# A gated two-mixer decoder layer on one core: which units of a gate block are seven-product units, how far ahead units are split, in how many steps a unit is rounded, and where token sums stand in the queues

## The chip, the cores and the metric

The kernel runs on one core of one Trainium2 chip. The metric is the device time of one execution in microseconds (us); lower is better. The kernel before takes 1052.6 us, the median of 3 runs (1051.69 to 1054.95).

## The reference

One decoder layer on 256 tokens of width 2048, all in float32. With `h` the normalised input, `proj = h @ w_in` is cut into the parts of two token mixers and two sets of merge gates:

```python
attn = attention(q, k, v) * silu(z_mla);          y_mla  = attn @ w_o_mla
conv = causal_conv(c_gate * c_in)                 # three taps
y_conv = (b_gate * conv * silu(z_conv)) @ w_o_conv
merged = sigmoid(g_mla) * y_mla + sigmoid(g_conv) * y_conv
out = x + rmsnorm(merged @ w_out) * g
```

`g_mla` and `g_conv` are each a product of the 256 x 2048 input with a 2048 x 2048 matrix of weights. The change is about these two products, the *gate stage*, and about the work shortly ahead of it.

## The kernel before, in words

**Numbers as pairs.** Every float32 operand is held as a rounded part and a remainder. ScalarE (ACT in the profile) makes the rounded copy, and VectorE (DVE) subtracts it from the source to get the remainder (`split_act`: lines 268 and 269). A product is three matmuls: high by high, high by low, low by high (`product`).

**Units.** The weights come as a list of units of 128 x 2048 numbers, one MB each, numbered in the order of use. SyncE (SP) loads them into three buffers `raw`. ACT writes `whi`, DVE writes `wlo`, each with three buffers; TensorE (PE) reads those. So `whi` of unit j goes where that of unit j - 3 was, and can be written when PE has finished unit j - 3. `raw` of unit j is loaded when DVE has done the remainder of unit j - 3. `take(i)`, called where PE's work on unit i is written, first calls `ahead`: it writes down loads and splits of the units that follow. In the gate stage and up to the last column block of the output it goes two units ahead with splits, elsewhere one.

**Order.** Matmuls, and those instructions that are wrapped in `keep_in_program_order`, keep the order in which the code is written, each on its engine. Everything else is placed by a scheduler of the framework, which may move an instruction forward in its engine's queue where another is expected to be ready later. Each engine then works its queue strictly in that order.

**Heads.** For each of 16 heads `h` (0 to 15) PE runs the scores of the head (`sc`), four units of convolution channels (`channels(h, 0..3)`, tile `cv`), the attention values of the head before (`o`), and every other head the queries and keys of the next pair of heads (`qn`, `kn`). At the end of `channels(h, 3)` the PSUM banks `cv` are read by ACT and DVE (`cv_w` or `cv_f`, lines 731 to 736).

**Token sums.** `token_sums` (lines 782 to 798), called in head 13 behind the keys of heads 14 and 15, adds and subtracts slices of the input (`xf`, six DVE instructions) and splits the four results (`xs`). The gate stage reads `xs`.

**Gate stage.** It has four blocks: `n` is the gate, `b` the half of its columns. A block has eight units, and a unit is of one of two kinds. A *whole* unit needs 24 matmuls (eight products). A *pair* unit needs seven products, 21 matmuls, by a scheme of the Strassen-Winograd kind: for it `split_pair` makes three sums of weight blocks on DVE: `tf` (1024 wide), `raw` (512 wide, it overwrites the first quarter of the raw unit), `tf` again (512 wide), at line 212. Then come the rounded copy and the remainder of the unit itself (`whi`, `wlo`) and of the three sums (`thi`, `tlo`, one buffer each). PE's products on a pair unit go in the order 7, 5, 1, 6, 4, 2, 3: the first two read `thi` and `tlo`, and product 4, the fifth in order, is the last that reads them. `gate_kinds` says which of the eight places is which: blocks 1 to 3 have pairs at places 0, 2, 4; block 0 has them at places 2, 4, 6.

After the last pair of a block ACT copies two product banks (`p1`, `p5`) and DVE forms the sums `u`. At the end of the block DVE adds and ACT applies the sigmoid (`sg`, lines 980 and 981).

Of the kernel before, what the change touches and what calls it, by code (L numbers as in the profile page):

```python
# [11 lines left out]
F32 = mybir.dt.float32  # L12
F32R = mybir.dt.float32r
I32 = mybir.dt.int32
AF = mybir.ActivationFunctionType
# [8 lines left out]
H = 16  # L24
# [60 lines left out]
def tile_layer(ctx: ExitStack, tc: tile.TileContext, xw, x, pos, pvec, post_g, wc, wz, wcv, wkr, wqk, wqr, wv, cwr, wsq, wg, out):  # L85
# [118 lines left out]
    def split_pair(i, t, hi, lo):  # L204

        raw = t[:, :].rearrange("p (b c) -> p b c", b=4)
        tf = d0.tile([P, 2, 3, S], F32, name=f"tf{i}", tag="tf", bufs=1)[:, :, :, :].rearrange("p a b c -> p (a b c)")
        tf = tf.rearrange("p (b c) -> p b c", b=3)
        thi, tlo = (d1.tile([P, 3, 512], F32R, name=f"t{o}{i}", tag=f"t{o}", bufs=1) for o in ("hi", "lo"))

        def tt(*a, op):
            tc.keep_in_program_order(nc.vector.tensor_tensor(*a, op=op))
# [54 lines left out]
    def split_act(hi, lo, src, keep=False):  # L267
        a = nc.scalar.activation(hi, src, AF.Copy)  # L268
        b = nc.vector.tensor_tensor(lo, src, hi.bitcast(F32), op=ALU.subtract)  # L269
        if keep:  # L270

            tc.keep_in_program_order(a)
            tc.keep_in_program_order(b)
# [508 lines left out]
    def token_sums(pool):  # L782


        both = x_both[:, :, :].bitcast(F32).rearrange("p (g k) c -> p g k c", k=STEP)[:, :2, :PAIRS]
        xs = pool.tile([P, 4, PAIRS, 2, P], F32R, name="xs")
        xf = pool.tile([P, 2, PAIRS, S], F32, name="xf", tag="tf", bufs=1)
        tt = nc.vector.tensor_tensor
        for g in range(2):
            tt(xf[:, g], both[:, g, :, :S], both[:, g, :, S:], op=ALU.add)  # L790
        (a11, a21), (a12, a22) = [[xf[:, g, :, t * P : (t + 1) * P] for t in range(NT)] for g in range(2)]
        tt(a22, a21, a22, op=ALU.add)
        tt(a21, a11, a21, op=ALU.subtract)
        tt(a11, a22, a11, op=ALU.subtract)
        tt(a12, a12, a11, op=ALU.subtract)
        for i, f in enumerate((a22, a11, a21, a12)):
# [12 lines left out]

    dstack = main.enter_context(ExitStack())  # L810

    for h in range(H):
        v, at = divmod(h, HV)

# [50 lines left out]
        if at and h < H - 1:  # L865
            arrive()
        channels(h, 2)
        if at == 0:
            arrive()
            if v:  # L870
                coming.append(channels_join(v - 1, 0))
# [6 lines left out]
        if h == H - 3:  # L878
            lstack.close()
            d0 = dstack.enter_context(tc.tile_pool(name="d0", bufs=1))  # L880
            xs = token_sums(d0)
        channels(h, 3)
        if at == 0:
            while coming:
                arrive()
# [50 lines left out]
    def gate_block(n, b, last):  # L936
# [17 lines left out]
        for i, (kind, ks) in enumerate(kinds):  # L954
            if last:
                for v in {6: (0, 1), 7: (2,)}.get(i, ()):
                    split_branch(v)
            w = take(units[i])
            if kind == "pair":
                for m in TAGS:  # L960
                    if m:
                        add_to(m, side(m, ks[0]), w[m], i, True)
            else:
                for m, t, half in ((2, 0, 0), (3, 0, 1), (4, 1, 0), (0, 1, 1)):
                    for j, k in enumerate(ks):
                        a = [x_both[:, k, o + t * P : o + (t + 1) * P] for o in (0, S)]
                        add_to(m, a, w(2 * j + half, 512), i, j == len(ks) - 1)
            if i == last_pair:
                p1, p5 = wide("p1"), wide("p5")
# [134 lines left out]

def gate_kinds():

    pairs = [("pair", (k, k + STEP)) for k in range(PAIRS)]
    paired = {k for _, ks in pairs for k in ks}
    rest = [k for k in range(KD) if k not in paired]
    plain = [("whole", ks) for ks in zip(rest[::2], rest[1::2])]  # L1110
    alternate = []
    for i, pair in enumerate(pairs):
        alternate += [pair, plain[i]]
    alternate += plain[PAIRS:]
    late = plain[-2:] + [u for u in alternate if u not in plain[-2:]]
    return {(n, b): late if n == b == 0 else alternate for n in range(2) for b in range(2)}


def _cols(w):
# [99 lines left out]
```

## Time and profile before

| | |
|---|---|
| median of 3 runs | 1052.6 us |
| the profiled execution | 1052.53 us |
| its span, first to last instruction | 1050.7 us |
| DVE busy | 743.0 us, 71% |
| ACT busy | 532.5 us, 51% |
| matmuls recorded | 4658 |
| granted PE clock, mean | 0.991 |
| gate stage on PE | 606.65 to 781.69 us of the span |

A row of a timeline has the start in us, the duration in us, the engine, the line, the operation, what is written and read, the shapes, and how many such instructions follow one another; in brackets stands how long the engine was idle and what ended that. Matmuls are pipelined: one of 128 x 512 has a duration of 0.39 us, and the next can start 0.23 us after it, so delays are read from the distance between starts. A row of grouped instructions has the count, the busy time, the mean duration in ns, and the idle time ahead of them with what ended it. A row of waits has total us, times, longest.

### The profile page before, as it was taken

The page shows a single profiled execution, that of the slowest core. Times are in us where ns is not written, and L with a number is a line of the kernel's source. Part 1 is how long each engine was busy: PE and PEld are TensorE (multiplying, and loading weights), DVE is VectorE, ACT ScalarE, POOL GpSimd, SP SyncE. Part 2 cuts the span into 40 slices and gives each one's busy share as a digit, 9 for nine tenths or more (in the row PEclk, how much of TensorE's full clock was granted, in tenths as well). Part 3 has the DMA queues.
Part 4 walks back from the last instruction along what each step waited for, and adds up shares of the span by engine and source line. Part 5 has one row for each costly group of instructions (what it writes and reads, how often), then busy time and mean ns, then how long its engine had stood idle before and what let it go on. Part 6 is the DMA issues. An engine that isn't in the chain of part 4 may idle for free.

```text
span 1050.7 us, 12467 instructions
## 1 busy us (share of the span) xinstructions
PE 1026.5 (98%) x4658; PEld 852.6 (81%) x4658; DVE 743.0 (71%) x960; ACT 532.5 (51%) x675; POOL 180.7 (17%) x345
## 2 busy tenths in 40 slices
PE   9999999999999999999998999899999999999997
PEld 7887888888888888888886878688888888888885
DVE  7578759677687767777776799788885545666562
ACT  7766546455555455564553545555564433333451
POOL 7621220204212142112312220000000000232000
PEclk9999999999999999999998999899999999999998
DMA  8754765668666685765765765455555555677842
GB/s 337 295 199 177 257 212 212 226 214 275 197 243 195 226 284 199 244 216 203 264 231 196 248 216 186 165 194 202 200 206 195 199 200 192 220 252 247 330 160 80
DMA packets 41948, 231.00 MB, mean 220 GB/s; under 512 B 7520, under 2 KB 8224, under 8 KB 18976
## 3 DMA queue, kind: packets, MB, share of 16 engines
q1 hardware_dynamic: 29808, 197.54, 52.8%
q0 software_dynamic: 11648, 29.38, 9.1%
q10 hardware_dynamic: 432, 3.29, 0.8%
q8 instruction: 36, 0.59, 0.2%
q14 instruction: 24, 0.20, 0.0%
HBM read 214.48 MB, written 11.53 MB: 215 GB/s over the span
## 4 chain that ended last, share of the span: by engine, by line
PE 83%; DVE 9%; issue 4%; ACT 2%; DMA 1%; SPq 0%; DVEq 0%; ACTq 0%
PE cv L90 28%; PE sq L90 17%; PE g L90 10%; PE z L90 8%; PE out L90 8%; DVE wlo L269 4%; PE qn L90 2%; PE ckv L90 2%; ACT whi L268 2%; PE kn L90 2%; PE qa L90 2%; PE vv L90 2%; PE sc L90 1%; PE o L90 1%; DVE tlo L269 1%
## 5 line engine op out<-in xcount | busy, mean ns | idle before, releaser
L269 DVE TENSOR_TENSOR wlo<-raw,whi 128x1024 fp32r<-128x1024 f32 (+2 forms) x290 | 423.5, 1485 | 229.0 <-ACT whi L268 228.4
L268 ACT ACTIVATE whi<-raw 128x1024 fp32r<-128x1024 f32 (+2 forms) x292 | 357.3, 1259 | 373.8 <-PE sq L90 96.9
L90 PE MATMUL cv<-whi,x_both 128*128 128x512 f32 x1024 | 324.1, 391 | 2.7 <-DVE cv_w L736 2.7
L90 PEld LDWEIGHTS cv<-whi,x_both 128*128 128x128 f32 x1024 | 192.9, 188 | 43.1 <-DVE cv_w L736 3.7
L90 PE MATMUL cv<-wlo,x_both 128*128 128x512 f32 x512 | 200.2, 391 | 0.0
L90 PE MATMUL g<-whi,x_both 128*128 128x512 f32 x368 | 119.8, 390 | 0.0
L90 PEld LDWEIGHTS cv<-wlo,x_both 128*128 128x128 f32 x512 | 96.4, 188 | 18.8
L90 PEld LDWEIGHTS g<-whi,x_both 128*128 128x128 f32 x368 | 69.5, 189 | 14.6
L90 PE MATMUL z<-whi,x_both 128*128 128x512 f32 x256 | 80.6, 390 | 0.0
L90 PE MATMUL sq<-whi,x_both 128*128 128x512 f32 x256 | 79.0, 389 | 0.0
L90 PE MATMUL sq<-whi,cv_both 128*128 128x512 f32 x256 | 79.0, 389 | 0.0
L90 PE MATMUL out<-whi,x_both 128*128 128x512 f32 x256 | 79.0, 389 | 0.0
L355 POOL DMA_DIRECT2D far<-via x64 | 35.3, 559 | 225.8 <-DVE via L348 224.8
L90 PE MATMUL g<-wlo,x_both 128*128 128x512 f32 x184 | 71.8, 390 | 0.0
L355 POOL DMA_DIRECT2D far<-sg x32 | 17.5, 552 | 311.5 <-DVE sg L1025 270.2
L90 PEld LDWEIGHTS sq<-whi,x_both 128*128 128x128 f32 x256 | 48.0, 188 | 10.0
L90 PEld LDWEIGHTS sq<-whi,cv_both 128*128 128x128 f32 x256 | 48.0, 188 | 9.9
L90 PEld LDWEIGHTS out<-whi,x_both 128*128 128x128 f32 x256 | 48.0, 188 | 9.9
L90 PEld LDWEIGHTS z<-whi,x_both 128*128 128x128 f32 x256 | 48.1, 188 | 9.9
L90 PE MATMUL z<-wlo,x_both 128*128 128x512 f32 x128 | 49.8, 389 | 0.0
L90 PE MATMUL sq<-wlo,x_both 128*128 128x512 f32 x128 | 49.8, 389 | 0.0
L90 PE MATMUL sq<-wlo,cv_both 128*128 128x512 f32 x128 | 49.8, 389 | 0.0
(242 smaller groups left out, 1327.6 us busy)
## 6 DMA issues: line engine op xcount, KB each, us to landing
raw<-wcv_dram SPq DMA_DIRECT2D x64, 1024.0 KB, 5.4
raw<-wsq_dram SPq DMA_DIRECT2D x48, 1024.0 KB, 4.8
raw<-wg_dram SPq DMA_DIRECT2D x32, 1024.0 KB, 4.7
raw<-wz_dram SPq DMA_DIRECT2D x16, 1024.0 KB, 4.8
raw<-wqk_dram SPq DMA_DIRECT2D x8, 1024.0 KB, 6.7
cw<-cwr_dram POOLq DMA_DIRECT2D x24, 256.0 KB, 6.3
raw<-wc_dram SPq DMA_DIRECT2D x4, 1024.0 KB, 10.0
raw<-wv_dram SPq DMA_DIRECT2D x4, 1024.0 KB, 5.3
```

The lines of the kernel that those rows point to most:

```text
L90: return tc.keep_in_program_order(nc.tensor.matmul(*a, **kw))
L268: a = nc.scalar.activation(hi, src, AF.Copy)
L269: b = nc.vector.tensor_tensor(lo, src, hi.bitcast(F32), op=ALU.subtract)
L355: tc.keep_in_program_order(nc.gpsimd.dma_start(out=f[i], in_=m))
```

## The change

Five edits, in places that meet in the same queues:

- `gate_kinds`: block 0 has its pairs at places 3 and 5, two instead of three; blocks 1 to 3 keep theirs at 0, 2, 4. So 11 of 32 units are pairs, not 12.
- `take`: one unit ahead with splits and three with loads everywhere, also in the gate stage.
- `split_pair`: the rounded copy of the unit is made in two steps: 1536 columns that no sum overwrites, written down ahead of the sums, and the first 512 behind them. Its remainder is written down behind the split of the sums.
- `token_sums` becomes a generator that is called step by step in head 14, behind `channels` 1, 2 and 3, with its sums and splits pinned to program order.
- After the last pair, `p5` is gone: DVE reads product 5 from its PSUM bank, in two instructions of 512 columns instead of one of 1024.

```diff
@@ split_pair
+        nc.scalar.activation(hi[:, 512:], t[:, 512:], AF.Copy)
         tt(tf[:, :2], raw[:, 1:3], raw[:, 0:1].to_broadcast([P, 2, 512]), op=ALU.subtract)
         tt(raw[:, 0], raw[:, 2], tf[:, 0], op=ALU.add)
         tt(tf[:, 2], raw[:, 3], raw[:, 0], op=ALU.subtract)
-        split_act(hi[:, :], lo[:, :], t[:, :])
+        nc.scalar.activation(hi[:, :512], t[:, :512], AF.Copy)
         split_act(thi[:, :, :], tlo[:, :, :], tf[:, :, :])
+        nc.vector.tensor_tensor(lo[:, :], t[:, :], hi[:, :].bitcast(F32), op=ALU.subtract)
@@ take
-        far_ahead = u_g[0][0] <= i < u_out[3, 0]
-        ahead(i, raw=3 + far_ahead, split=1 + far_ahead)
+        ahead(i)
@@ token_sums
+        yield xs
         for g in range(2):
             tt(xf[:, g], both[:, g, :, :S], both[:, g, :, S:], op=ALU.add)
+            yield
...
         for i, f in enumerate((a22, a11, a21, a12)):
-            split_act(xs[:, i, :, 0], xs[:, i, :, 1], f)
-        return xs
+            split_act(xs[:, i, :, 0], xs[:, i, :, 1], f, True)
+            if i % 2:
+                yield
@@ heads: behind channels(h, 1), channels(h, 2) and channels(h, 3)
+        if h == H - 2:
+            next(sums)
+            next(sums)
@@ gate_block
-                nc.scalar.activation(p5[:, :], ps[5][:, :], AF.Copy)
...
-                tt(u[:, :2], u[:, 0::2], p5[:, :].rearrange("p (o c) -> p o c", o=1).to_broadcast([P, 2, 512]), op=ALU.subtract)
+                for o in (1, 0):
+                    tt(u[:, o], u[:, 2 * o], ps[5][:, :], op=ALU.subtract)
@@ gate_kinds
+    for block in range(4):
+        at = (0, 2, 4) if block else (3, 5)
+        pairs = [(k, k + STEP) for k in range(len(at))]
...
+            ("pair", pairs[at.index(i)]) if i in at else ("whole", next(left)) for i in range(KD // 2)
```

The queues of POOL and SP are the same row by row, apart from the numbers of the tiles; PE's has one pair less. DVE's and ACT's differ in three stretches. On DVE, where the keys `kn` of heads 14 and 15 are split, the queue before reads (the number in a name is that of the tile; `xf`, `xs` are the token sums, `f` holds a key product before its split, `wlo` a unit's remainder):

```order
L422 TENSOR_TENSOR f_4877<-kn7_0_4859,half_4878 128x256
L422 TENSOR_TENSOR f_4883<-kn7_1_4860,half_4884 128x256
L736 SCALAR_TENSOR_TENSOR cv_f_114<-cv13_0_4706,r_both_105,cv_f_114 128x512
L793 TENSOR_TENSOR xf_4894<-xf_4894 128x3x128
L736 SCALAR_TENSOR_TENSOR cv_f_114<-cv13_1_4707,r_both_105,cv_f_114 128x512
L269 TENSOR_TENSOR xs_4893<-xf_4894,xs_4893 128x3x128
L269 TENSOR_TENSOR wlo107_5027<-raw107_4989,whi107_5026 128x1024
L794 TENSOR_TENSOR xf_4894<-xf_4894 128x3x128
L269 TENSOR_TENSOR wlo107_5027<-raw107_4989,whi107_5026 128x1024
L269 TENSOR_TENSOR kn_4820<-f_4877,kn_4820 128x256
```

and the changed one, at the same place:

```order
L423 TENSOR_TENSOR f_4877<-kn7_0_4859,half_4878 128x256
L423 TENSOR_TENSOR f_4883<-kn7_1_4860,half_4884 128x256
L737 SCALAR_TENSOR_TENSOR cv_f_114<-cv13_0_4706,r_both_105,cv_f_114 128x512
L270 TENSOR_TENSOR kn_4820<-f_4877,kn_4820 128x256
L270 TENSOR_TENSOR kn_4820<-f_4883,kn_4820 128x256
L737 SCALAR_TENSOR_TENSOR cv_f_114<-cv13_1_4707,r_both_105,cv_f_114 128x512
L270 TENSOR_TENSOR wlo107_5013<-raw107_4975,whi107_5012 128x1024 x2
L791 TENSOR_TENSOR xf_4894<-x_both_109 128x768 x2
```

Between `f` and `kn` one instruction is left of seven, and the token sums stand behind the next unit's remainder. In head 14 the queue of DVE ahead of the read of the `cv` banks of that head is now:

```order
L270 TENSOR_TENSOR wlo110_5196<-raw110_5136,whi110_5195 128x1024
L349 STREAM_TRANSPOSE via_5081<-p_5063 128x3x4x32
L770 TENSOR_TENSOR mv1_4929<-mv1_4929,cw_4935 128x512
L770 TENSOR_TENSOR mv2_4932<-mv2_4932,cw_4937 128x512
L270 TENSOR_TENSOR wlo110_5196<-raw110_5136,whi110_5195 128x1024
L737 SCALAR_TENSOR_TENSOR cv_w_620<-cv14_0_4973,r_both_105,cv_w_620 128x512
L770 TENSOR_TENSOR mv1_4929<-mv1_4929,mv2_4932 128x512
```

Before, both halves of `wlo110` stood behind `mv2`, and the joining `mv1` stood ahead of `cv_w`. The third place is the second pair of block 1, unit 123, where DVE's queue before reads:

```order
L980 TENSOR_TENSOR sg_5376<-g00_0_5384,u_5626 128x512
L212 TENSOR_TENSOR tf123_5682<-raw123_5632 128x1024
L212 TENSOR_TENSOR raw123_5632<-raw123_5632,tf123_5682 128x512
L212 TENSOR_TENSOR tf123_5682<-raw123_5632 128x512
L269 TENSOR_TENSOR wlo123_5681<-raw123_5632,whi123_5680 128x2048
L269 TENSOR_TENSOR wlo124_5716<-raw124_5678,whi124_5715 128x2048
L269 TENSOR_TENSOR tlo123_5684<-tf123_5682,thi123_5683 128x1536
```

and the changed one, from the remainder of the sums of unit 121 on:

```order
L270 TENSOR_TENSOR tlo121_5620<-tf121_5618,thi121_5619 128x1536
L1000 TENSOR_TENSOR sg_5376<-g00_2_5382,p1_5577 128x512
L270 TENSOR_TENSOR wlo122_5672<-raw122_5614,whi122_5671 128x2048
L1000 TENSOR_TENSOR sg_5376<-g00_3_5383,u_5578 128x512
L212 TENSOR_TENSOR tf123_5700<-raw123_5669 128x1024
L1000 TENSOR_TENSOR sg_5376<-g00_4_5381,u_5578 128x512
L1000 TENSOR_TENSOR sg_5376<-g00_0_5384,u_5578 128x512
L212 TENSOR_TENSOR raw123_5669<-raw123_5669,tf123_5700 128x512
L212 TENSOR_TENSOR tf123_5700<-raw123_5669 128x512
L220 TENSOR_TENSOR wlo123_5699<-raw123_5669,whi123_5698 128x2048
L270 TENSOR_TENSOR wlo124_5738<-raw124_5696,whi124_5737 128x2048
L270 TENSOR_TENSOR tlo123_5702<-tf123_5700,thi123_5701 128x1536
```

The first sum has moved ahead of two `sg`; the remainder `wlo123` still stands ahead of `tlo123`, though the code writes it behind, and so does `wlo124`. In the other pairs of the changed kernel the order on DVE is `tf`, `raw`, `tf`, `wlo`, `tlo`, with the next unit's `wlo` behind them.

More of the change, by code (lines that the diff above doesn't have):

```diff
@@ L793, in token_sums @@
         tt(a21, a11, a21, op=ALU.subtract)
+        yield
         tt(a11, a22, a11, op=ALU.subtract)
         tt(a12, a12, a11, op=ALU.subtract)
+        yield
         for i, f in enumerate((a22, a11, a21, a12)):
-            split_act(xs[:, i, :, 0], xs[:, i, :, 1], f)
-        return xs
+            split_act(xs[:, i, :, 0], xs[:, i, :, 1], f, True)
+            if i % 2:
+                yield
     cv_w = bp.tile([P, NT, 512], F32, name="cv_w")
@@ L810, in tile_layer @@
     dstack = main.enter_context(ExitStack())
+    sums = None
     for h in range(H):
@@ L867, in tile_layer @@
         channels(h, 2)
+        if h == H - 2:
+            next(sums)
+            next(sums)
         if at == 0:
@@ L880, in tile_layer @@
             d0 = dstack.enter_context(tc.tile_pool(name="d0", bufs=1))
-            xs = token_sums(d0)
+            sums = token_sums(d0)
+            xs = next(sums)
         channels(h, 3)
+        if h == H - 2:
+            next(sums)
+            next(sums)
         if at == 0:
@@ L968, in gate_block @@
             if i == last_pair:
-                p1, p5 = wide("p1"), wide("p5")
+                p1 = wide("p1")
                 u = d1.tile([P, 3, 512], F32, name="u", tag="u", bufs=1)
                 nc.scalar.activation(p1[:, :], ps[1][:, :], AF.Copy)
-                nc.scalar.activation(p5[:, :], ps[5][:, :], AF.Copy)
                 tt = nc.vector.tensor_tensor
@@ L1105, in gate_kinds @@
 def gate_kinds():
[L1107 to L1116, printed above, removed]
+    kinds = {}
+    for block in range(4):
+        at = (0, 2, 4) if block else (3, 5)
+        pairs = [(k, k + STEP) for k in range(len(at))]
+        paired = {k for ks in pairs for k in ks}
+        rest = [k for k in range(KD) if k not in paired]
+        left = iter(zip(rest[::2], rest[1::2]))
+        kinds[divmod(block, 2)] = [
+            ("pair", pairs[at.index(i)]) if i in at else ("whole", next(left)) for i in range(KD // 2)
+        ]
+    return kinds
 def _cols(w):
```

3 lines of the change are left out of this document (2 added, 1 removed).

## The prediction

> **What bounds the kernel now.** I read the page first, then what TensorE (PE) waits for, then PE's timeline at each wait, then DVE's and ACT's timelines ahead of those.
>
> ```profile
> PE 1026.5 (98%) x4658; PEld 852.6 (81%) x4658; DVE 743.0 (71%) x960; ACT 532.5 (51%) x675; POOL 180.7 (17%) x345
> ...
> PE sc L90 <- DVE kn L269: 5.8, 1, 5.8
> PE g L90 <- DVE tlo L269: 4.1, 3, 2.5
> PE cv L90 <- DVE cv_w L736: 2.7, 4, 0.8
> ```
>
> PE is the bound: it is busy 98% of the span, and its few waits are all for remainders or bank reads of DVE. So a gain can only be fewer matmuls or shorter waits, and the rest of the span goes at the pace of an undisturbed stretch:
>
> ```profile
> 770.36 0.39 PE L90 MATMUL g<-wlo,x_both 128*128 128x512 f32 x1
> ...
> 781.69 0.39 PE L90 MATMUL sq<-whi,x_both 128*128 128x512 f32 x1
> ```
>
> 50 matmuls start from the first of these to the second: 11.33 us, 0.2266 us each. A whole unit (24) is 5.44 us, a pair (21) is 4.76 us.
>
> Now the waits that the change can reach, by the starts of matmuls; the first two rows are an undisturbed passage from channels over scores to channels, four heads earlier:
>
> ```profile
> 415.06 0.39 PE L90 MATMUL cv<-whi,x_both 128*128 128x512 f32 x1
> ...
> 416.23 0.39 PE L90 MATMUL cv<-whi,x_both 128*128 128x512 f32 x1
> ...
> 550.63 0.39 PE L90 MATMUL cv<-whi,x_both 128*128 128x512 f32 x1
> ...
> 558.61 0.63 PE L90 MATMUL cv<-whi,x_both 128*128 128x512 f32 x1
> ...
> 560.74 0.66 PE L90 MATMUL cv<-whi,x_both 128*128 128x512 f32 x2
> ```
>
> Undisturbed the passage takes 1.17 us; ahead of the scores of head 14 it takes 7.98, and the five matmuls after it, 0.43 apart, 2.13 where five times 0.2266 is 1.13. Lost: 6.81 + 1.00 = 7.8 us, 5.8 of it the wait itself and 2.0 a slow clock behind it.
>
> ```profile
> 582.75 0.39 PE L90 MATMUL cv<-whi,x_both 128*128 128x512 f32 x1
> 583.58 0.50 PE L90 MATMUL cv<-whi,x_both 128*128 128x512 f32 x1 [0.43 <-DVE cv_w L736]
> ...
> 627.77 0.39 PE L90 MATMUL g<-thi,xs 128*128 128x512 f32 x1
> 629.27 0.50 PE L90 MATMUL g<-tlo,xs 128*128 128x512 f32 x1 [1.11 <-DVE tlo L269]
> ...
> 659.60 0.39 PE L90 MATMUL g<-whi,x_both 128*128 128x512 f32 x1
> ...
> 663.98 0.80 PE L90 MATMUL g<-tlo,xs 128*128 128x512 f32 x1 [2.52 <-DVE tlo L269]
> ...
> 670.08 0.39 PE L90 MATMUL g<-whi,x_both 128*128 128x512 f32 x1
> ...
> 718.39 0.39 PE L90 MATMUL g<-thi,xs 128*128 128x512 f32 x1
> 719.22 0.50 PE L90 MATMUL g<-tlo,xs 128*128 128x512 f32 x1 [0.45 <-DVE tlo L269]
> ```
>
> With 0.23 taken off for the matmul itself: 0.6 us at 582.75, 1.3 at 627.77, 0.6 at 718.39. From 659.60 to 670.08 sixteen matmuls start, 3.63 us of work in 10.48: 6.85 us lost, of which 3.9 are waits (659.60 to 663.98, two matmuls) and 2.9 a slow clock. All together 17.15 us; apart from these five places PE runs at its pace, so this is the most that waits can give.
>
> **The change part by part.** *One pair less.* 21 whole units instead of 20 and 11 pairs instead of 12: three matmuls more, +0.68 us on the path for certain.
>
> *Token sums.* Why PE waited before head 14 stands on DVE's timeline; the last two rows are the same place four heads earlier:
>
> ```profile
> 545.59 1.83 DVE L790 TENSOR_TENSOR xf<-x_both 128x768 f32<-128x768 f32 x2 [0.47 <-PE kn L90]
> ...
> 550.07 0.56 DVE L792 TENSOR_TENSOR xf<-xf 128x384 f32<-128x384 f32 x1
> 550.54 0.75 DVE L422 TENSOR_TENSOR f<-kn,half 128x256 f32<-128x256 f32 x2
> 551.20 0.75 DVE L736 SCALAR_TENSOR_TENSOR cv_f<-cv,r_both,cv_f 128x512 f32<-128x512 f32 x1
> ...
> 556.19 0.76 DVE L269 TENSOR_TENSOR kn<-f,kn 128x256 fp32r<-128x256 f32 x2
> ...
> 412.91 0.74 DVE L422 TENSOR_TENSOR f<-kn,half 128x256 f32<-128x256 f32 x2
> ...
> 414.24 0.75 DVE L269 TENSOR_TENSOR kn<-f,kn 128x256 fp32r<-128x256 f32 x2
> ```
>
> The new queue has the order of 412.91: `f`, `cv_f`, `kn`, nothing else. There `kn` starts 1.33 us after `f`, and `f` 2.38 us ahead of the matmul at 415.29 (one after 415.06). Without `xf` in front (1.83 and 0.56), `f` starts some 2.1 us earlier, at 548.4, `kn` at 549.8, done by 550.5; PE wants the first of the two at 550.86. I count the whole 7.8 us as gone. What is late next is 0.4 us away, so a small rest is possible; a loss beyond before is excluded, since no row was added ahead of `kn`.
>
> The sums do not vanish: 1.83 us and eight of 0.56, 6.3 us of DVE work, now lie in head 14, where DVE must also read the `cv` banks in time. This is the chain there before:
>
> ```profile
> 577.74 2.01 ACT L268 ACTIVATE whi<-raw 128x1024 fp32r<-128x1024 f32 x2 [0.33 <-PE cv L90]
> ...
> 578.23 0.58 DVE L348 STREAM_TRANSPOSE via<-p 128x384 f32<-128x384 f32 x1
> 578.73 1.25 DVE L769 TENSOR_TENSOR mv<-mv,cw 128x512 f32<-128x512 f32 x2
> 579.90 2.36 DVE L269 TENSOR_TENSOR wlo<-raw,whi 128x1024 fp32r<-128x1024 f32 x2
> ...
> 582.77 0.75 DVE L736 SCALAR_TENSOR_TENSOR cv_w<-cv,r_both,cv_w 128x512 f32<-128x512 f32 x1
> ```
>
> In the new queue one half of `wlo` stands ahead of `via`. It can't start before PE frees the buffer of `whi110`, one unit (5.44 us) before PE wants the bank. From there: 0.2 to the start of ACT, 1.0 for half of `whi`, then on DVE 1.13, 0.5, 1.17, 1.13 and 0.75 = 5.9 us. PE waits 0.45 us instead of 0.6. The bounds: nothing, if the buffer is seen free at once, and 6.3 us, all of the sums' work. On ACT the exponentials of head 14 now stand behind a `whi` that waits for PE's buffer; behind them waits `pt`, which PE wants a head later, so I take nothing for that.
>
> *Gate stage.* The prices of its steps, as groups over 606 to 782 us:
>
> ```profile
> L269 DVE TENSOR_TENSOR wlo<-raw,whi 128x2048 fp32r<-128x2048 f32 x32 | 73.0, 2288 | 21.4 <-ACT whi L268 21.4
> L269 DVE TENSOR_TENSOR tlo<-tf,thi 128x1536 fp32r<-128x1536 f32 x12 | 21.0, 1750 | 1.5 <-ACT thi L268 1.5
> L212 DVE TENSOR_TENSOR tf<-raw 128x1024 f32<-128x1024 f32 x12 | 14.6, 1220 | 0.1
> L212 DVE TENSOR_TENSOR raw<-raw,tf 128x512 f32<-128x512 f32 x12 | 8.3, 692 | 0.4
> ...
> L980 DVE TENSOR_TENSOR sg<-g,u 128x512 f32<-128x512 f32 x12 | 7.7, 686 | 0.0
> ...
> L268 ACT ACTIVATE whi<-raw 128x2048 fp32r<-128x2048 f32 x33 | 62.9, 1913 | 62.1 <-DVE raw L212 41.3 <-PE g L90 13.5 <-issue 7.3
> L268 ACT ACTIVATE thi<-tf 128x1536 fp32r<-128x1536 f32 x12 | 17.7, 1474 | 2.6 <-DVE wlo L269 2.3 <-DVE tf L212 0.2
> ```
>
> Of the 21.4 us in which DVE stood before a `wlo`, much is a pair's: ACT waits for `raw` (41.3 us), then copies 2048 columns while DVE has nothing. The new first step of 1536 columns needs no sum. The second, of 512, isn't in the trace: between 0.44 us (the difference of the two ACT rows) and 1.47; I take 0.6, near the difference. It runs beside DVE's last sum (0.69), so `wlo` starts when the sums end, 1.4 us earlier in each pair. ACT has 62 us of idle time in the stage for the extra instruction, and is rid of the `p5` copies.
>
> Starts on DVE follow about 0.08 us closer than durations say (`mv`, 1.25, is followed after 1.17). Walk the pairs from there. In block 0 two whole units come first, and the second pair (place 5) has its `thi` buffer free at the fifth product of the first pair: 3.4 us into it, so 6.8 us before PE wants it. Then 0.2, `thi` 1.4 and `tlo` 1.7: ready with 3 us to spare; the 1.3 us go. In blocks 2 and 3 the pair behind a pair's whole unit is bound in the same way, with the 1.4 us to spare against a wait of 0.6: that goes too.
>
> Unit 123, the second pair of block 1, is the crowded one. Count from the start of the last pair of block 0 on PE, when the buffer for `whi120` is free: 0.2 and 1.9 on ACT. Then DVE has no gap: `wlo120`; `tf`, four `u` and two more sums (seven instructions, six of them 512 wide); `wlo121`, `tlo121`, one `sg`, `wlo122`, three `sg` among three sums, `wlo123`, `wlo124`, `tlo123`. That is five of 2.21 (11.05), two of 1.67 (3.34), two of 1.2 (2.4), and twelve 512 wide at about 0.64 (7.7): 24.5, together 26.6 us. PE is there after two whole units, a pair, a whole unit and the last pair's own 4.76: 25.84, plus 0.23 until it wants `tlo`. It waits about 0.5 to 0.8 us; I take 0.7 for the 6.85. Before, it waited 3.9: the last pair stood one place later, so PE had a whole unit less to do meanwhile, and the 1.4 us lay ahead of `wlo123`. With 1.47 for the small copy it would be 1.5; with no pauses between dependent steps, 0.
>
> The copies `p5` were ACT's, off the path; the two reads from PSUM in their place, at the 686 of `sg`, add 0.15 us to DVE and are in the count. Loads need 4.7 us, and their queue keeps its order:
>
> ```profile
> raw<-wg_dram SPq DMA_DIRECT2D x32, 1024.0 KB, 4.7
> ```
>
> Each waits for the `wlo` three units back, and by the same walk no chain finds its `raw` less than 3 us early. Splitting one ahead instead of two costs nothing by itself: with three buffers the split of unit j can't start before PE starts unit j - 2, whichever number `take` gives; it only moves other work ahead of a split.
>
> A page of the Trainium skill, "TensorE: Matmul & The Clock Gate", Part 1 on the clock gate, says that PE drops to half its clock after about 3.4 us of idleness and needs as long busy to come back. The trace agrees on when: 5.8 and 3.9 us of waiting left slow matmuls, 0.6 to 1.3 us did not. By that rule each slow spell costs 1.7 us, an estimate from that page, 3.4 for both where the rows show 2.0 + 2.9; the sum would then be 1.5 us smaller and the time 1038.7. I keep the rows.
>
> **The sum.** 7.8 + 0.6 + 1.3 + 6.85 + 0.6 = 17.15 us gone, 0.45 + 0.7 + 0.68 = 1.83 back: 15.3 us. The profiled execution took 1052.53 us (span 1050.7 and 1.8 around it), 0.1 below the median of the runs: 1037.2 us.
>
> **The rivals.** *Clean:* both small waits are covered: 1.15 us less, 1036.1. For it: both come out of sums with 0.3 to 0.7 us of play. Chance 0.15.
>
> *Unit 123 stays late:* `wlo124` and its ACT copy still stand ahead of `tlo123`. If the wait stays at 3.9 with its slow spell of 2.9, 1037.2 + 6.8 - 0.7 = 1043.3. It begins where the wait passes the 1.3 us that left the clock alone. Chance 0.13.
>
> *The sums return in head 14:* DVE is full there from `kn` to `cv_w`, and all 6.3 us land on PE: 1043.5. Against it: the waits for exponentials and copies leave DVE idle there now. Chance 0.10.
>
> *It does not do what it says:* `wlo` still precedes `tlo`, and if the copies are no earlier the three gate waits stay: 1037.2 + 8.75 - 0.7 = 1045.3. Chance 0.06.
>
> *Slower: one ahead is too late.* If a pair's split starts only when PE starts the unit ahead of it, the chain of 1.22 + 0.69 + 0.69 + 2.29 + 2.29 + 1.75 = 8.9 us meets 5.44: 3.5 us late, eleven times, 1036.1 + 38 = 1074. It beats the gain from 1.5 us per pair on. Against it: the queue puts a pair's first sum directly behind the split before it, with nothing of PE's in between. Chance 0.04.
>
> **How the numbers follow.** The forecast keeps 0.52. The range runs from below the clean case to above the two single returns, 1035.0 to 1044.0, and leaves out the last two rivals. A measurement of this kernel tells about 0.3% (3 us) from no change: faster 0.95 (all but the last), same 0.01, slower 0.04.
>
> **What would show it.** In the profile after: scores of head 14 start 0.23 us after the last `cv`, with no PE wait on `kn`; a wait on `cv_w` under 1 us at the end of head 14; in the gate stage one wait, on `tlo` at the second pair of block 1, under 1.5 us, and no slow matmuls; 735 matmuls of the gates instead of 732. Wrong would be: a wait on `tlo` at every pair, any slow spell, or waits on `raw`.

## The result and the profile after

The changed kernel takes 1037.4 us, the median of 4 runs (1036.97 to 1037.89), against 1052.7 us of the kernel before on the same chip (1051.69 to 1054.95): a ratio of 0.985, 95% interval 0.9835 to 0.9869. The profiled execution took 1037.89 us, with a span of 1036.1 us and a mean granted clock of 0.998.

The page of the kernel after, first its row of busy times, then the row of the granted clock over 40 slices:

```profile
PE 1022.2 (99%) x4661; PEld 851.2 (82%) x4661; DVE 738.4 (71%) x960; ACT 530.6 (51%) x681; POOL 180.9 (17%) x345
...
PEclk9999999999999999999999999999999999999999
```

Three matmuls more, and PE is busy for 4.3 us less: the slow matmuls behind the two long waits are gone from its busy time, and no slice of the clock row is below 9 (in the row before, slices 22 and 26, where the two long waits lie, are at 8, as is the last). What PE still waits for, in the view of waits (total us, times, longest):

```profile
PE cv L90 <- DVE cv_w L737: 2.9, 4, 0.9
...
PE g L90 <- DVE tlo L270: 0.4, 1, 0.4
```

The wait of 5.8 us on `kn` has left the list (what is left out here are two rows of the start, 1.7 and 1.1 us), and of the 4.1 us on `tlo` 0.4 is left. PE's timeline at the three places of interest: the scores of head 14, the end of that head, and unit 123:

```profile
551.53 0.39 PE L90 MATMUL cv<-whi,x_both 128*128 128x512 f32 x1
551.76 0.28 PE L90 MATMUL sc<-kn,qn_hi 128*128 128x256 f32 x1
...
575.80 0.39 PE L90 MATMUL cv<-whi,x_both 128*128 128x512 f32 x1
576.62 0.50 PE L90 MATMUL cv<-whi,x_both 128*128 128x512 f32 x1 [0.43 <-DVE cv_w L737]
...
652.14 0.39 PE L90 MATMUL g<-thi,xs 128*128 128x512 f32 x1
652.91 0.50 PE L90 MATMUL g<-tlo,xs 128*128 128x512 f32 x1 [0.39 <-DVE tlo L270]
653.25 0.62 PE L90 MATMUL g<-thi,xs 128*128 128x512 f32 x2
```

The first score starts 0.23 us after the last `cv`: nothing is lost there. With a matmul's own 0.23 taken off, 0.59 us are lost at 575.80 and 0.55 (unrounded) at 652.14, and in both places the matmul behind the wait takes 0.11 longer (652.91 to 653.25 is 0.34). No other stretch from head 12 to the end of the gates is late.

On DVE, where the keys are split, the queue is `f`, `cv_f`, `kn`:

```profile
549.38 0.75 DVE L423 TENSOR_TENSOR f<-kn,half 128x256 f32<-128x256 f32 x2
550.04 0.74 DVE L737 SCALAR_TENSOR_TENSOR cv_f<-cv,r_both,cv_f 128x512 f32<-128x512 f32 x1
550.70 0.75 DVE L270 TENSOR_TENSOR kn<-f,kn 128x256 fp32r<-128x256 f32 x2
...
646.45 2.29 DVE L220 TENSOR_TENSOR wlo<-raw,whi 128x2048 fp32r<-128x2048 f32 x1
648.90 2.29 DVE L270 TENSOR_TENSOR wlo<-raw,whi 128x2048 fp32r<-128x2048 f32 x1 [0.16 <-ACT whi L269]
651.11 1.75 DVE L270 TENSOR_TENSOR tlo<-tf,thi 128x1536 fp32r<-128x1536 f32 x1
```

The `kn` are done at 551.45, 0.3 us ahead of PE. The lower rows are unit 123: its `wlo`, that of unit 124, and only then `tlo`, done at 652.86.

DVE's and ACT's groups of rows over the gate stage (599 to 776 us), with the idle time ahead of each in the last column; the pairs' `wlo` now have line 220:

```profile
L220 DVE TENSOR_TENSOR wlo<-raw,whi 128x2048 fp32r<-128x2048 f32 x11 | 25.2, 2291 | 2.7 <-ACT whi L218 2.7
```

```profile
L218 ACT ACTIVATE whi<-raw 128x512 fp32r<-128x512 f32 x11 | 6.9, 623 | 3.9 <-DVE raw L212 3.9
```

The small copy takes 0.62 us (0.6 was taken), and DVE stands only 2.7 us before the remainders of eleven pairs.

### The profile page after: what moved, and what is told of

Read it like the earlier page. It is cut to its first block, busy times and chain, and to the rows that moved or that the text cites. A ratio compares the mean times of both kernels' runs of the same rounds, so it can differ in the third digit from the quotient of the medians.

```text
span 1036.1 us, 12480 instructions
## 1 busy us (share of the span) xinstructions
PE 1022.2 (99%) x4661; PEld 851.2 (82%) x4661; DVE 738.4 (71%) x960; ACT 530.6 (51%) x681; POOL 180.9 (17%) x345
## 4 chain that ended last, share of the span: by engine, by line
PE 95%; DVE 3%; issue 1%; ACT 1%; DVEq 0%; POOL 0%; POOLq 0%
PE cv L90 32%; PE sq L90 17%; PE g L90 16%; PE z L90 8%; PE out L90 8%; PE qa L90 2%; PE qn L90 2%; PE ckv L90 2%; PE kn L90 2%; PE vv L90 2%; DVE wlo L270 1%; PE sc L90 1%; PE o L90 1%; PE qr L90 1%; ACT whi L269 0%
## 5 line engine op out<-in xcount | busy, mean ns | idle before, releaser
L270 DVE TENSOR_TENSOR wlo<-raw,whi 128x1024 fp32r<-128x1024 f32 (+2 forms) x279 | 398.5, 1452 | 213.3 <-ACT whi L269 212.3
L269 ACT ACTIVATE whi<-raw 128x1024 fp32r<-128x1024 f32 (+2 forms) x281 | 336.4, 1233 | 344.2 <-issue 104.9
L90 PE MATMUL g<-whi,x_both 128*128 128x512 f32 x380 | 122.4, 389 | 0.0
L90 PE MATMUL g<-wlo,x_both 128*128 128x512 f32 x190 | 73.9, 389 | 0.0
```

The lines of the kernel that those rows point to most:

```text
L90: return tc.keep_in_program_order(nc.tensor.matmul(*a, **kw))
```

## The experiments

The theory: DVE was late for PE at five places, and each edit removes its own share: the token sums 7.8 us, the places and the two-step copy the rest; splitting one ahead and the two reads of product 5 do next to nothing. The first rival: the edits aren't separate, what one is worth depends on the others. The second: the order in which the scheduler puts remainders, and not the amount of DVE's work, is what decides at the pairs. All times below stand against the kernel before on the same chip (1052.5 to 1052.7 us), and 1037.4 us is the changed kernel.

**Undoing one edit: the token sums.** `token_sums` is called whole in head 13, as before, and its instructions are no longer pinned.

```diff
-            split_act(xs[:, i, :, 0], xs[:, i, :, 1], f, True)
+            split_act(xs[:, i, :, 0], xs[:, i, :, 1], f)
...
-            sums = token_sums(d0)
-            xs = next(sums)
+            xs = token_sums(d0)
```

> The changed kernel with the token sums as before, called in one go in head 13 and free to be placed. The walk says that the scores of head 14 wait 5.8 us for the keys again, with 2.0 us of slow clock behind that: 7.8 us more, 1045.2 us, and the gate stage as in the changed kernel. The rival, that the sums' 6.3 us of VectorE work only moved and cost something in head 14 now, says less: 2 us or so more, 1039 us, with the wait on the cv banks of head 14 falling well below its 0.6 us.

Measured: 1045.3 us, ratio 0.993 (0.9912 to 0.9945). The view of waits of this run:

```profile
PE sc L90 <- DVE kn L270: 5.7, 1, 5.7
```

The wait is back, slow matmuls behind it, 7.9 us in all. The wait on `cv_w` at the end of head 14 stayed at 0.59 us: the sums that lie there now do not make it longer.

**Undoing one edit: the copy in one step.**

```diff
-        nc.scalar.activation(hi[:, 512:], t[:, 512:], AF.Copy)
...
-        nc.scalar.activation(hi[:, :512], t[:, :512], AF.Copy)
+        split_act(hi[:, :], lo[:, :], t[:, :])
...
-        nc.vector.tensor_tensor(lo[:, :], t[:, :], hi[:, :].bitcast(F32), op=ALU.subtract)
```

This also writes the remainder of the unit ahead of the split of the sums again, as before the change; the run doesn't part the two.

> The changed kernel with the rounded copy of a pair unit in one step, behind the sums. The walk says that each pair's remainder starts 1.4 us later; all pairs but unit 123 have 2 to 3 us to spare, so only its wait grows, from 0.55 to about 2 us: 1038.8 us. The rival, that the two steps are what frees the gate stage, says that the waits at the second pair of block 0 (1.3), at unit 123 (3.9, with a slow clock) and in block 2 (0.6) come back: up to 8 us more, 1045 us.

Measured: 1039.8 us, ratio 0.988 (0.9861 to 0.9891), 2.4 us more. DVE's timeline at unit 123:

```profile
646.69 4.49 DVE L268 TENSOR_TENSOR wlo<-raw,whi 128x2048 fp32r<-128x2048 f32 x2 [1.40 <-ACT whi L267]
651.10 1.75 DVE L268 TENSOR_TENSOR tlo<-tf,thi 128x1536 fp32r<-128x1536 f32 x1
```

DVE stands 1.40 us before the remainder of unit 123, and PE loses 1.70 there instead of 0.55, with the clock untouched. The second wait (0.55 us, in block 2) was not expected: there the scheduler again puts the next unit's `wlo` ahead of the `tlo` that PE wants, as in the kernel before. With the slower matmul behind it, this wait and the longer one at unit 123 make 1.8 of the 2.4 us.

**Undoing one edit: splits two ahead.**

```diff
-        ahead(i)
+        far_ahead = u_g[0][0] <= i < u_out[3, 0]
+        ahead(i, raw=3 + far_ahead, split=1 + far_ahead)
```

> The changed kernel with splits two units ahead in the gate stage, as before. The walk says that the lead itself is worth nothing, since the buffers allow a split no earlier; but the queue of VectorE has all sums u ahead of the sums of unit 121 and its tlo behind two sg, so that unit 121 waits about 1.2 us, and unit 123, whose tlo now stands ahead of the next wlo, no longer waits: 1038.0 us. The rival, that one ahead is what removed the waits, says waits of several us at pairs of all blocks: 1041 us or more.

Measured: 1038.1 us, ratio 0.986 (0.9848 to 0.9878), 0.8 us more, which is no more than the runs of one kernel scatter. The trace shows a cause of that size: the wait moves from unit 123 to unit 121, the first pair of block 1, and is 1.25 us long. On DVE's timeline `wlo122` and `sg` now stand ahead of `tlo121`:

```profile
637.80 2.28 DVE L271 TENSOR_TENSOR wlo<-raw,whi 128x2048 fp32r<-128x2048 f32 x1
640.00 0.69 DVE L1001 TENSOR_TENSOR sg<-g,u 128x512 f32<-128x512 f32 x1
640.60 1.75 DVE L271 TENSOR_TENSOR tlo<-tf,thi 128x1536 fp32r<-128x1536 f32 x1
```

**Undoing one edit: the places.** Block 0 has its three pairs at 2, 4, 6 again (`gate_kinds` as before).

> The changed kernel with the pairs of block 0 at places 2, 4, 6 as before: 12 pairs, three matmuls less (0.68 us). The walk says that unit 117 no longer waits, but that the sums u of block 0 come one whole unit later and stand with three sg and two remainders ahead of tlo of unit 121, which is ready some 6 us late, with a slow clock of 2 to 3 us behind it: about 1045 us. The rival, that the places don't matter and a pair more is a plain gain, says 1036.7 us.

Measured: 1046.0 us, ratio 0.994 (0.9923 to 0.9953), 8.6 us more although PE has three matmuls less. The waits on `tlo` (total, times, longest):

```profile
PE g L90 <- DVE tlo L270: 6.3, 3, 5.2
```

The long one is at unit 121 (5.46 us from start to start, and 0.70 for `thi` one matmul earlier), with slow matmuls behind it. Two small ones, 0.88 and 0.59 us at the first two pairs of block 0, were not expected; they are explained two runs below.

**Undoing one edit: product 5.** ACT copies it again, and DVE subtracts 1024 columns in one instruction.

> The changed kernel with product 5 copied by ACT again and one subtraction of 1024 columns on DVE. My theory: off the path except ahead of unit 123, where the two reads from PSUM cost 0.15 us of DVE: its wait goes from 0.55 to 0.4 us, the time is 1037.2 us, no difference that shows. Rival: the copy of product 5 on ACT stands ahead of a whi or thi that PE or DVE waits for, or holds the PSUM bank longer or shorter: more than 1 us either way, with a new wait at the end of a block.

Measured: 1037.2 us, ratio 0.985 (0.9839 to 0.9868), no difference. The wait at unit 123 stayed at 0.55 us, so that even the 0.15 us of DVE's work does not show.

**One edit alone: the token sums.** The kernel before with the generator, pinned, in head 14.

```diff
+        def tt(*a, op):
+            tc.keep_in_program_order(nc.vector.tensor_tensor(*a, op=op))
...
+        if h == H - 2:
+            next(sums)
+            next(sums)
```

> The kernel before with only the token sums called step by step in head 14 and pinned. My theory: PE's wait on the keys and the slow clock behind it (7.8 us) go, nothing else moves: 1044.9 us, with the wait on the cv banks at the end of head 14 at 0.6 us. Rival: the 7.8 us are worth less alone than together, since the gate stage then starts with DVE later than before by the 6.3 us of sums, and unit 123 or the first pair waits longer: 1048 us or more.

Measured: 1046.3 us, ratio 0.994 (0.9919 to 0.9952): 6.3 us, not 7.8. The wait on `kn` is gone, but the first pair of block 0 now waits 0.58 us and the second 2.00 instead of 1.27. The reason stands on DVE's timeline in head 15, where it waits for data that POOL's queue loads (`cw`, the weights of the convolution):

```profile
593.04 0.69 DVE L769 TENSOR_TENSOR mv<-mv,cw 128x512 f32<-128x512 f32 x1 [0.55 <-DMA cw<-cwr_dram]
595.25 0.69 DVE L769 TENSOR_TENSOR mv<-mv,cw 128x512 f32<-128x512 f32 x1 [1.52 <-DMA cw<-cwr_dram]
...
596.59 2.29 DVE L269 TENSOR_TENSOR wlo<-raw,whi 128x2048 fp32r<-128x2048 f32 x1
```

and the kernel before at that place:

```profile
600.08 1.29 DVE L769 TENSOR_TENSOR mv<-mv,cw 128x512 f32<-128x512 f32 x2
...
602.79 2.29 DVE L269 TENSOR_TENSOR wlo<-raw,whi 128x2048 fp32r<-128x2048 f32 x1 [0.70 <-ACT whi L268]
```

PE is 7.67 us earlier here (575.08 against 582.75 at the end of head 14), so the `wlo` of 602.79 would be due at 595.12; it starts 1.47 later. Why the load is later stands on POOL's timeline of this run:

```profile
583.84 0.55 POOL L753 DMA_DIRECT2D mv<-cv_f  x1
...
585.38 1.09 POOL L753 DMA_DIRECT2D cw<-cwr_dram  x2
```

and of the kernel before:

```profile
590.62 1.09 POOL L753 DMA_DIRECT2D cw<-cwr_dram  x2
```

The loads of `cw` stand behind transfers of `cv_f`, which DVE finishes behind the four pinned `xs`; 590.62 less 7.67 is 582.95, so they go out 2.4 us later than due. So the sums did return a part, one head and one stage on: 1.3 us at two pairs. In the changed kernel the same two waits for `cw` are in the trace (0.82 and 1.27 us), but its first pair stands one unit later, and PE meets none of it. In the run with the old places they are 0.82 and 1.54 us, and its first pair stands at place 2: from the `wlo` behind them (597.05) to the end of its second pair's `tlo` (622.04) DVE stands idle nowhere. I read its two small waits as the same thing. The expectation had the place of the loss in its rival, and twice its size.

**One edit alone: the copy.** The kernel before with the change's part of `split_pair`, the later place of the remainder included.

> The kernel before with only the rounded copy of a pair in two steps; pairs, splits two ahead and token sums as before. My theory: the copy frees 1.4 us of DVE per pair, so the wait of 1.3 us at the second pair of block 0 goes, the 0.6 us in block 2 goes, and the 3.9 us at unit 123 becomes 2.5. If 2.5 us of waiting leaves the clock alone, the 2.9 us of slow matmuls go as well: 1052.7 - 1.3 - 0.6 - 1.4 - 2.9 = 1046.5 us. If 2.5 us is enough for a slow clock: 1049.4 us, with matmuls 0.43 us apart behind the wait. I take the first. Rival: the remainder of the sums still stands behind the remainder of the unit and the next unit's, so the copy moves nothing that PE waits for, and the gain is under 1 us: 1051.7 us or more. The 7.8 us ahead of the scores of head 14 stay in either case.

Measured: 1049.8 us, ratio 0.997 (0.996 to 0.9981). The forecast of 1046.5 fell: of 1.4 us the second pair of block 0 and unit 123 got 0.7 each, and the wait that is left there, 3.26 us, still had slow matmuls behind it (1.7 us). ACT's timeline ahead of unit 123 shows why,

```profile
654.68 1.92 ACT L270 ACTIVATE whi<-raw 128x2048 fp32r<-128x2048 f32 x1 [1.16 <-issue]
656.50 0.61 ACT L218 ACTIVATE whi<-raw 128x512 fp32r<-128x512 f32 x1
```

and DVE's, at the second pair of block 0 and at unit 123:

```profile
625.33 2.29 DVE L271 TENSOR_TENSOR wlo<-raw,whi 128x2048 fp32r<-128x2048 f32 x1 [0.61 <-ACT whi L270]
...
653.90 0.69 DVE L212 TENSOR_TENSOR raw<-raw,tf 128x512 f32<-128x512 f32 x1
...
657.14 2.29 DVE L220 TENSOR_TENSOR wlo<-raw,whi 128x2048 fp32r<-128x2048 f32 x1 [1.83 <-ACT whi L218]
```

The scheduler put the copy of unit 124 between the two steps: `raw` is done at 654.59, the second step begins at 656.50, and DVE stands idle for 1.83 us. In block 0 the `wlo` of the next unit, still ahead of `tlo`, waits for its own copy and eats half of the gain.

**One edit alone: the places,** then **places and token sums.**

> The kernel before with only the new places of the pairs (3, 5, then 0, 2, 4). My theory: the places are what frees unit 123, since PE has a whole unit more to do while DVE works on the end of block 0. The wait of 1.3 us in block 0 goes; at unit 123 the wait of 3.9 us becomes 1.7 to 2.0 (as in the run with the copy in one step) and leaves the clock alone, so 5.0 of the 6.85 us go; the 0.6 us in block 2 and the 7.8 us ahead of the scores of head 14 stay; three matmuls more cost 0.68: 1052.7 - 1.3 - 5.0 + 0.7 = 1047.0 us, in spite of one pair less. Rival: with splits two ahead and the copy in one step the wait at unit 123 stays over 3 us and keeps its slow matmuls: 1050.5 us or more.

Measured: 1051.4 us, ratio 0.9987 (0.9978 to 0.9996): 1.1 us, and the rival has it. DVE's timeline around the first two pairs of block 1:

```profile
644.95 2.29 DVE L269 TENSOR_TENSOR wlo<-raw,whi 128x2048 fp32r<-128x2048 f32 x1 [1.40 <-ACT whi L268]
...
657.49 4.50 DVE L269 TENSOR_TENSOR wlo<-raw,whi 128x2048 fp32r<-128x2048 f32 x2 [1.39 <-ACT whi L268]
661.90 1.75 DVE L269 TENSOR_TENSOR tlo<-tf,thi 128x1536 fp32r<-128x1536 f32 x1
```

and PE's:

```profile
660.68 0.50 PE L90 MATMUL g<-thi,xs 128*128 128x512 f32 x1 [0.76 <-ACT thi L268]
663.71 0.50 PE L90 MATMUL g<-tlo,xs 128*128 128x512 f32 x1 [2.52 <-DVE tlo L269]
```

The wait at unit 123 is 0.92 + 2.80 = 3.7 us instead of 3.9: the places alone do next to nothing for it. They remove the 1.3 us in block 0; at unit 123 PE loses 5.4 us instead of 6.9, nearly all of that difference because the slow spell behind the wait cost 1.7 instead of 2.9.

> The kernel before with the token sums in head 14 and the new places together. My theory: alone, the sums gave 6.3 us instead of 7.8, because DVE enters the gate stage about 1.5 us later and the pairs at places 2 and 4 of block 0 wait for it; with the first pair at place 3 that wait is covered, so here the sums give their 7.8 us in full: 7.8 us less than the run beside it, about 1039.2 us. Rival: the 1.5 us are carried through block 0 to unit 123, which then waits over 3 us with slow matmuls: 1041 us or more, and a difference of 6.5 us or less to the run beside it.

Measured: 1044.3 us, ratio 0.992 (0.99 to 0.9933). The forecast of 1039.2 fell with that of the places alone, on which it was built. No pair of block 0 waits, as the theory has it, and unit 123 waits 3.7 us with slow matmuls, as without the sums, so that the rival's reason, that the sums carry a delay to this place, fell too. Beside the run with the places alone the sums give 7.1 us, which lies between the two expectations; the slow spell at unit 123 cost 2.6 us here and 1.7 there, which is about as much as the sums fall short of 7.8.

**Trying to remove the rest: `tlo` first.** `wlo` of a pair pinned behind `tlo`, and on ACT the copy of the whole unit behind a pair pinned behind `thi`.

```diff
+            if u_g[0][0] < i <= u_g[-1][-1] and plan[i - 1][2] == "pair":
+                tc.keep_in_program_order(a)
...
-        split_act(thi[:, :, :], tlo[:, :, :], tf[:, :, :])
-        nc.vector.tensor_tensor(lo[:, :], t[:, :], hi[:, :].bitcast(F32), op=ALU.subtract)
+        split_act(thi[:, :, :], tlo[:, :, :], tf[:, :, :], True)
+        tt(lo[:, :], t[:, :], hi[:, :].bitcast(F32), op=ALU.subtract)
```

> The changed kernel with the remainder of a pair pinned behind the remainder of its sums on DVE, and the rounded copy of the whole unit behind a pair pinned behind the rounded sums on ACT. In the queues both remainders of whole units that stood ahead of the one that unit 123 waits for are now behind it. My theory: the wait of 0.55 us at unit 123 goes, and nothing is late in its place: by the walk tlo of unit 123 is done 1.5 us before PE wants it; 1036.8 us. Rival: the remainder of the pair itself, now later, is what PE waits for at product 1 (or a sg moved ahead of the sums makes a bank late): 1038 us or more, with a wait on wlo or on hi in blocks 1 to 3.

Measured: 1044.9 us, ratio 0.993 (0.9912 to 0.9942): 7.6 us worse than the changed kernel where 0.6 better was forecast. The waits, then ACT's timeline at the start of block 2:

```profile
PE g L90 <- DVE wlo L202: 2.8, 3, 1.4
...
PE g L90 <- DVE wlo L215: 1.6, 3, 0.6
```

```profile
683.95 2.02 ACT L1004 ACTIVATE sg<-sg,r_both 128x512 f32<-128x512 f32 x3 [4.63 <-DVE sg L1003]
686.60 0.72 ACT L1004 ACTIVATE sg<-sg,r_both 128x512 f32<-128x512 f32 x1 [0.64 <-DVE sg L1003]
687.23 1.90 ACT L201 ACTIVATE whi<-raw 128x2048 fp32r<-128x2048 f32 x1
```

The pinned copy had moved behind the four sigmoids of the block before, the last of which waits for PE's end of that block. In the changed kernel the copy of the same unit stands ahead of all four and starts at 678.91. Everything behind it is late: the whole unit's `wlo`, then `tlo` and `wlo` of the next pair.

**Other places.** The pairs of blocks 1 and 2 move too. In whole units between the last pair of a block and the first of the next, the changed kernel has 2, 3 and 3; this run has 4, 2 and 2, which is not what its expectation says (one more at every end). A second run has a third pair in block 0, at place 7, and with it 2, 2 and 2 (and a correction of where bank 0 is completed, which the pair at place 7 needs).

```diff
-        at = (0, 2, 4) if block else (3, 5)
+        at = ((3, 5), (2, 4, 6), (1, 3, 5), (0, 2, 4))[block]
```

> The changed kernel with the pairs at places 3, 5 in block 0, 2, 4, 6 in block 1, 1, 3, 5 in block 2 and 0, 2, 4 in block 3: as many matmuls, but at each end of a block three units instead of two from the last pair to the next. My theory: unit 123 waited because its split fell together with the sums and sg of block 0; now DVE has a whole unit (5.4 us) more there, the wait of 0.55 us (0.66 with the slower matmul behind it) goes and nothing is late instead: 1036.7 us, against 1037.4 of the changed kernel. Rival: the scheduler again puts the remainder of the next whole unit ahead of that of the sums at the first or second pair of a block, and the wait only changes its place: 1037.4 us or more, with a wait on tlo of 0.5 us or more in block 2 or 3.

Measured: 1043.2 us, ratio 0.991 (0.9895 to 0.9921), 5.8 us worse. The wait in block 1, which now comes four whole units behind the last pair, is gone. In block 2, behind two, one of 4.00 us takes its place, with nine slow matmuls (1.7 us). Block 3, where the places are as in block 1 of the changed kernel and behind the same two units, has the 0.55 of unit 123 again, at its second pair. The rival had the wait's new place; what stands ahead of it is not a remainder, as it said, but `sg`. DVE's timeline in block 2:

```profile
683.33 0.69 DVE L1000 TENSOR_TENSOR sg<-g,u 128x512 f32<-128x512 f32 x1 [0.67 <-PE g L90]
683.93 1.22 DVE L212 TENSOR_TENSOR tf<-raw 128x1024 f32<-128x1024 f32 x1
...
690.99 1.75 DVE L270 TENSOR_TENSOR tlo<-tf,thi 128x1536 fp32r<-128x1536 f32 x1
```

The scheduler put all four `sg` ahead of the first sum of the next pair. The last `sg` waits for PE's last matmul of the block, so the sum starts with 4.9 us to go until PE wants `tlo` at 688.80, and the chain to it is 8.8 us long (683.93 to 692.74).

> The same with a third pair in block 0, at place 7, so twelve pairs again (3, 5, 7 then 2, 4, 6 then 1, 3, 5 then 0, 2, 4). My theory: three matmuls less than the run beside it, 0.68 us, and no wait for tlo: 1036.0 us. Rival: with a pair as the last unit of block 0 its bank of product 2 is complete only three matmuls before the next block writes the bank again, so PE waits there for the first sg (0.4 us if DVE is free, up to 2.7 if a remainder of 2.29 us stands ahead of it): 1036.4 to 1038.7 us, with a wait on sg at the end of block 0.

Measured: 1049.5 us, ratio 0.997 (0.9961 to 0.9981). The rival's mechanism, and three times: PE waits for the banks that the `sg` of block 0 still read, 2.2, 2.1 and 1.3 us. The first of them on PE's timeline:

```profile
643.35 0.47 PE L90 MATMUL g<-whi,x_both 128*128 128x512 f32 x1 [2.05 <-DVE sg L1000]
```

A whole unit as the last of a block completes these banks one after another, six matmuls apart; a pair completes the last three of them in its last nine. The waits on `tlo` of the run before are here as well, 4.00 us in block 2, with a slow spell of 3.0, and 0.55 in block 3. No version tried is faster than the changed kernel by more than the runs scatter.

## Why the prediction was right, and where its reasons were not

**The sum.** 1037.2 us forecast, 1037.4 measured. By steps, in PE's starts: 7.8 + 1.3 + 0.6 us gone in full, 6.85 down to 0.55, 0.6 to 0.59, and three matmuls (0.68) added: 17.15 - 1.82 = 15.3 us. The span fell by 14.6 only, since PE is 0.75 us later already in head 10 of this trace (the passage that began at 415.06 begins at 415.81), ahead of all that the change touches. That forecast and result agree to 0.2 us is partly luck: the slow spells of 2.0 and 2.9 us were read from one execution, and in other runs such spells cost 1.7 to 3.0.

**Token sums, 7.8 us.** Right: undone, they cost 7.9. What the prediction didn't have is the delay of 1.5 us that the pinned sums carry into the gate stage by way of a load; the place of the first pair covers it.

**The wait on `cv_w`, 0.45.** Measured 0.59, the same as before. ACT's row shows the chain's start, and its DVE rows the rest:

```profile
570.78 2.01 ACT L269 ACTIVATE whi<-raw 128x1024 fp32r<-128x1024 f32 x2 [0.32 <-PE cv L90]
```

```profile
571.88 1.23 DVE L270 TENSOR_TENSOR wlo<-raw,whi 128x1024 fp32r<-128x1024 f32 x1 [0.64 <-ACT whi L269]
...
574.68 1.22 DVE L270 TENSOR_TENSOR wlo<-raw,whi 128x1024 fp32r<-128x1024 f32 x1
575.82 0.74 DVE L737 SCALAR_TENSOR_TENSOR cv_w<-cv,r_both,cv_w 128x512 f32<-128x512 f32 x1
```

The walk was right row by row; 0.10 us from the copy to DVE and 0.06 from DVE to PE were missing. That it equals the wait before is chance: the two chains hold different rows.

**Unit 123, 0.7 of 6.85.** The number was right (0.55), and so was the walk: from the start of block 0's last pair on PE (626.30) to the end of `tlo123` it takes 26.56 us, 26.6 forecast, against 26.07 when PE wants it. The reason given for the gain over before was wrong. The prediction said that PE has a whole unit more to do in this time; but DVE's chain grows by as much. The kernel before, from the first row to the end of the second:

```profile
639.42 0.39 PE L90 MATMUL g<-thi,xs 128*128 128x512 f32 x1
...
662.18 1.75 DVE L269 TENSOR_TENSOR tlo<-tf,thi 128x1536 fp32r<-128x1536 f32 x1
```

The same distance in the runs (start of the pair's first matmul, end of the `tlo` row; with the new places alone 633.89 to 663.65):

| kernel | from the last pair's start to `tlo123` | PE wants it at | PE loses there, slow matmuls included |
|---|---|---|---|
| before | 24.5 us | 20.6 | 6.9 |
| before, new places | 29.8 | 26.1 | 5.4 |
| changed, copy in one step | 27.7 | 26.1 | 1.7 |
| changed | 26.6 | 26.1 | 0.55 |

The new places alone leave 3.7 us of waiting. One ahead takes 2.1 us off the chain (the sums, which also differ between these two rows, leave it at 29.8, and the reads of product 5 at 26.6), 1.4 of it because the scheduler then puts sums of products (`u`) where DVE otherwise stands before `wlo121`. The copy takes 1.1 off. The clock makes the rest: 1.7 us of waiting leave it alone, 3.7 do not, so beside the places and the sums either edit is enough to end the slow spell (1039.8 with one ahead, 1038.1 with the copy, 1044.3 with neither), and undoing either one costs little.

**Splitting one ahead "costs nothing by itself".** True, and too little: it is worth 0.8 us with the two-step copy and 4.5 without (1044.3 against 1039.8, with the two reads of product 5 in the difference, which measured nothing). The 0.8 is within the runs' scatter, but the traces agree with it. No run has one ahead alone in the kernel before.

**The two-step copy, "1.4 us in each pair".** Right where no other copy stands between the steps (2.7 us of idle time are left over eleven pairs); in the kernel before one does at unit 123, and half of it is lost. In block 2 the prediction set 1.4 us against a wait of 0.6; `tlo` of that pair, the block's third, is ready 3.5 us ahead of PE, since the next unit's `wlo`, another 2.2 us, now stands behind it as well, which the prediction did not count. Whether the copy or the later place of the remainder in the code brings that order is open: no run parts them.

**The clock.** The Trainium skill, "TensorE: Matmul & The Clock Gate", Part 1 on the clock gate, has half the clock after some 3.4 us of idleness and as long a stretch until it is back, and says that this varies from run to run. The runs agree nearly: 2.2 us of waiting left the matmuls 0.23 us apart and 3.26 did not, a little below the figure of the Trainium skill, nor did 2.80 behind 0.92 with one matmul between them. A spell cost 1.7 us in three runs, as in the estimate by that rule, but after a wait of 4.00 us it cost 1.7 in one run and 3.0 in another.

**The rivals.** *Clean* did not come: both small waits stayed. That the sums return in head 14 fell by the first run: they return later, and smaller. That unit 123 stays late is what the kernel does with the places alone. That the edits do not do what they say fell: the gate waits of 8.75 us are down to 0.55. "One ahead is too late" did not happen in the changed kernel; its chain of 8.9 us against one unit is what the first run with other places shows, in block 2, where an `sg` ties the first sum to PE's end of a block.

## What to carry to other kernels

Take an edit's worth from the path with all other edits in, not alone: here the sums gave 6.3 us alone and 7.9 in company, the places 1.1 and 8.6, and the copy 2.8 and 2.4, because each changes who is late next and whether a wait is long enough for the slow clock. Where a scheduler places what isn't pinned, walk the queues that it makes, row by row from the event that frees the first buffer: that gave the small numbers here, and with `tlo` first, where the expectation gives a walk of DVE's queue and none of ACT's, the forecast failed. Pinning one more instruction to mend a queue can move it behind something that waits for the very engine that it should serve.

## What the runs showed of the hardware

Behind a wait of 0.55 to 2.1 us PE's next matmul took 0.34 instead of 0.23 us to the one after it, so that such a wait costs 0.11 us more than its own length. And the cost of a slow spell does not follow from the wait ahead of it: 1.7 us after waits of 3.26, 3.7 and 4.00, 2.6 after 3.7 and 6.2, 2.9 after 3.9, 2.8 after 4.1, 3.0 after another 4.00 (3.7, 3.9, 4.1 and 6.2 are each two waits with one matmul between). Four runs have the same wait of 5.7 to 5.8 us for the keys and lose the same in the scores behind it; the matmuls after the scores then lose 1.0 us in the kernel before, 1.25 with the sums undone, 1.5 with the places alone and 1.65 with the copy alone.
